# Stationary-weight products that keep to one kind of step for 32 steps instead of 16

## The chip, the cores and the metric

The kernel runs on one core of a Trainium2 chip. The metric is the device time of one execution in microseconds (us); lower is better. A core has five engines that work from queues of their own: PE (the tensor engine, with its weight loads shown apart as PEld), DVE (VectorE), ACT (ScalarE), POOL (GpSimd) and SP, which here only issues DMAs. An engine takes its instructions in the order in which the program put them, and waits on semaphores where it needs another's result.

## The reference

One encoder layer over 256 tokens of width 2048, in float32. Cut to what matters here:

```python
h = rms_norm(x, attn_norm)
qa, ka, va, qb, kb, vb, ga, gb = split(h @ w_in)
ya = windowed_gqa(qa, ka, va, ...)
yb = dilated_attention(qb, kb, vb, ...)
merged = sigmoid(ga) * (ya @ w_branch_a) + sigmoid(gb) * (yb @ w_branch_b)
x = x + merged @ w_out
hf = rms_norm(x, ffn_norm)
g = dwconv_centred(hf @ w_ffn_gate, conv_w, conv_b)
x = x + (gelu(g) * (hf @ w_ffn_up)) @ w_ffn_down
x = x + sigmoid(rms_norm(x, ple_norm) @ w_ple_gate) * (p @ w_ple_proj)
return rms_norm(x, final_norm)
```

The weights are the bulk of the input: all of them are read from memory once, and each is used for 256 tokens.

## The kernel before

**Numbers in two halves.** Products are made in a rounded float32 (fp32r). To keep the precision, each operand is split in two: a high half, the rounded value, and a low half, what the rounding lost. A product is high x high + high x low + low x high.

**Where the halves come from.** The weights are stored as one long stream of blocks of 128 x 128, in the order of use. SP's queue loads them (L265) into six raw buffers; a buffer holds a piece of eight blocks. `split_to(i)` (L276) makes the halves of the pieces up to number i: ACT copies the raw piece, rounding it, into `whi` (L288), and DVE subtracts that from the raw one into `wlo` (L289). `whi` and `wlo` have four buffers each, so the halves of piece s + 4 go where those of piece s were. `load_all` keeps the loads five to six pieces ahead of the split.

**The products with stationary weights.** `product` (L379) makes 128 columns of the q, k, gate (g) or up (u) projections: 16 blocks, two pieces. The weight block is loaded into PE and the activations stream past it. A **high step** (L396) takes a block of `whi` against both halves of the activations, 512 columns; a **low step** (L399) takes a block of `wlo` against their high half, 256 columns, and adds to the second half of the same accumulator. For each piece `eight` (L385) runs eight high and eight low steps: the first piece of a product high ones first, the second low ones first. So the order of kinds in a product is 8 high, 16 low, 8 high, and with the next product behind it, the high ones join to 16. At the start of each piece `split_to(s + 3)` asks for the halves of two pieces ahead. There are 115 such products among the 1840 steps of each kind: q and k ahead of and among the attention, three gate products, and the gate and up products in turn, in two halves of the MLP with the down projection between them.

**The gate products by halves.** The first three gate products (`products_by_halves`, L403) run side by side: the first piece of all three, then the second piece of all three, because the last features are finished only then. The first pieces are all high-first, the second ones low-first.

**What else stands in the order.** `run_due(i, k)` runs what was left for job i at count k: in a product, k goes from 0 to 15, one count for two steps. The scores of an attention head (`scores`, L696) stand at count 9 of the job after its last projection, the transposes of its normalized scores (`turn`, L739) at count 11 or 12 one job later. In the MLP, DVE and ACT work off each finished product: `gather` (L517, L513) adds the accumulator's halves; for a gate product the convolution follows (L846, L849), for every second up product the product with the gate and the sums for the down projection (L860, L863, L873 to L879). DVE also adds up quarters of later weights (`sums_of_quarters`, L322) that POOL's queue loads for it two jobs ahead. A scheduler places the instructions of each engine by its own estimates, so the order on DVE is not quite that of the code.

All other products (the value projections, the branch, output, down and embedding gates) have moving weights (L424 to L426, L475 to L477) and are not touched.

Of the kernel before, what the change touches and what calls it, by code (L numbers as in the profile page):

```python
# [17 lines left out]
T = 256  # L18
# [19 lines left out]
SUB = 8  # L38
# [102 lines left out]
def _pairs(kind, c):  # L141

    if kind == "pgs":
        return [0, 1, 4, 5, 2, 6, 7, 3], range(4, 8)
    if kind == "v8":
        return [0, 1, 2, 4, 3, 5, 6, 7], FARS
    if kind == "gab":
        return [0, 4, 1, 2, 6, 3, 5, 7], GATED
    if kind == "o":
        return ([2, 4, 5, 6, 7, 0, 1, 3] if c else [0, 1, 2, 4, 5, 6, 7, 3]), range(LATER, LATER + 4)  # L150
    if kind == "d1" and c == 1:
        return [5, 0, 1, 6, 2, 3, 7, 4, 8, 9, 10], range(5)
    return [8, 0, 1, 2, 3, 9, 4, 5, 6, 7, 10], range(SAVED)
# [38 lines left out]
def _whole(a):  # L192

    if _BLOCKS[a][0] == "w_in":
        return a == _SEVEN[3]
    pair, first = _BLOCKS[a + SUB][1] % FHALF // 2, not _BLOCKS[a + SUB][2]
    return _BLOCKS[a][0] in ("w_out", "w_ple_gate") or pair in WHOLE or (first and pair == 1)
# [15 lines left out]
_SUB_OF = {a + o: (i, o) for i, (a, n, part) in enumerate(_SUBS) if not part for o in range(n)}  # L213
# [3 lines left out]
def _encoder(ctx: ExitStack, tc, xt, pt, cols, table, onehot, mask, ident_in, last_gain, wts, xrows, out):  # L217
    nc = tc.nc
# [33 lines left out]

    raws, subs = {}, {}
    pairs_of, kept = {}, {}
    state = {"raw": 0, "sub": 0, "at": 0, "back": 0}
    held = {}

    def load(r, a=0, b=PIECE):
# [9 lines left out]
    def load_all(i):  # L268
        while state["raw"] < min(i, 2 * _NPIECES):
            r, h = divmod(state["raw"], 2)  # L270
            seven = h and r * PIECE in _SEVEN
            load(r, h * SUB, h * SUB + (4 if seven else SUB))
            if seven and _whole(r * PIECE):
                nc.sync.dma_start(raws[2 * r + h][:, 4:, :], kept[_SEVEN.index(r * PIECE)][1])

    def split_to(i):  # L276
        while state["sub"] < min(i, len(_SUBS)):
            s = state["sub"]
            a, n, part = _SUBS[s]
            h, o = divmod(a, SUB)  # L280
            load_all(h + 6 + (part == 3))
            if part is None:
                src = raws[h][:, o:min(o + n, SUB), :]
            else:
                src = (raws[h + 1][:, :4, :], pairs_of.get(a), raws[h], raws[h + 1])[part]
            hi = wpool.tile(list(src.shape), FR, name="whi", bufs=4)
            lo = wpool.tile(list(src.shape), FR, name="wlo", bufs=4)
            nc.scalar.activation(hi, src, AF.Copy)  # L288
            ins = nc.vector.tensor_tensor(lo, src, hi.bitcast(F32), op=ALU.subtract)  # L289
            if a // PIECE * PIECE in _EIGHT:  # L290
                keep(ins)
            subs[s] = (hi, lo)
            state["sub"] = s + 1
            if part is not None:
                t2, t4 = raws[h + 1][:, 4:, :], raws[h + 1][:, :4, :]
            if part == 0 and not _whole(a):
                keep(nc.vector.tensor_tensor(t2, raws[h][:, :4, :], pairs_of[a][:, :4, :], op=ALU.add))
            if part == 1:
                keep(nc.vector.tensor_tensor(t4, raws[h][:, 4:, :], t2, op=ALU.add))
                j = _SEVEN.index(a)  # L300
                if all(not j <= e < j + (3 if j > _ENDS["gab"] else 2) for e in _LAST):
                    back()
# [49 lines left out]
    def back():  # L352

        j = state["back"]
        t = two_sums() if "ff" in held else ap_.tile([P, SUB, P], F32, name="sums", tag="near", bufs=2)
        pairs_of[_SEVEN[j]] = t
        nc.sync.dma_start(t, kept[j][0])
        state["back"] = j + 1
# [19 lines left out]

    def product(i, moving, n):  # L379
        acc = ps.tile([P, 2 * T], F32, name="acc", bufs=3)  # L380
        for g in range(n // SUB):
            eight(acc, lambda k: run_due(i, SUB * g + k), lambda k: moving(SUB * g + k), g == 0, g == n // SUB - 1)
        return acc

    def eight(acc, due_at, moving, first, last):  # L385

        s, _ = _SUB_OF[state["at"]]
        for p in range(2 * SUB):
            if p % 2 == 0:
                due_at(p // 2)  # L390
                split_to(s + 3)
            hi, lo = subs[s]
            k = p % SUB
            m = moving(k)
            if (p < SUB) == first:
                nc.tensor.matmul(acc, hi[:, k, :], m, start=(first and k == 0), stop=(last and k == SUB - 1),  # L396
                                 skip_group_check=True)
            else:
                nc.tensor.matmul(acc[:, T:], lo[:, k, :], m[:, :T], start=False, stop=False, skip_group_check=True)  # L399
        state["at"] += SUB  # L400
        del subs[s]

    def products_by_halves(i, moving):  # L403

        accs = []
        for g in range(2 * TOGETHER):
            h, e = divmod(g, TOGETHER)
            if h == 0:
                tag = "sp" if e < 2 else "acc"
                accs.append(ps.tile([P, 2 * T], F32, name="acc", tag=tag, bufs=2 if e < 2 else 3))  # L410
            eight(accs[e], lambda k: run_due(i, SUB * g + k), lambda k: moving(SUB * h + k), h == 0, h == 1)
        return accs

    def wide_product(i, still, n, w, tag, places=HALVES, late=0):

        accs = [ps.tile([P, W4], F32, name="acc", tag=tag, bufs=3 if tag == "acc" else 2) for _ in places]

        def step(k, t, hi, lo):
            xh, xl = (still(k)[:, c:c + T][:, places[t]] for c in (0, T))
            acc = accs[t][:, :w * P]
            nc.tensor.matmul(acc, xh, hi, start=(k == 0), stop=False)  # L424
            nc.tensor.matmul(acc, xh, lo, start=False, stop=False)  # L425
            nc.tensor.matmul(acc, xl, hi, start=False, stop=(k == n - 1 - t * late))  # L426

        later = []
        for k in range(n):
            run_due(i, k)  # L430
            b = state["at"]
            s, o = _SUB_OF[b]
            split_to(s + 3)
            hi, lo = (m[:, o:o + w, :] for m in subs[s])
            step(k, 0, hi, lo)
            if k < n - late:
                step(k, 1, hi, lo)
            else:
                later.append((k, 1, hi, lo))
            state["at"] = b + w  # L440
            if o == _SUBS[s][1] - w:
                del subs[s]
        def rest(side=None):
            acc, c = (accs[1][:, :T], 0) if side is None else (side, T // P)
            for e, (k, t, hi, lo) in enumerate(later):
                xh, xl = (still(k)[:, c:c + T][:, places[t]] for c in (0, T))
                for i, (xs, ws) in enumerate(((xh, hi), (xh, lo), (xl, hi))):
                    nc.tensor.matmul(acc, xs, ws[:, c:c + T // P, :], start=(side is not None and e + i == 0),  # L448
                                     stop=(e + i == len(later) + 1), skip_group_check=True)
        return accs, rest  # L450
# [133 lines left out]
    def run_due(*i):  # L584
        for f, a in due.pop(i, []):
            f(*a)
# [554 lines left out]
    for i, job in enumerate(_JOBS):  # L1141
        kind, n, _, _, _, blocks = job
# [99 lines left out]
        last = i == len(_JOBS) - 1  # L1242
        rest = None
        if kind == "v":
            acc, _ = wide_product(i, stills["v"], blocks, len(n), "acc")
        elif kind in ("o", "d0", "d1", "gab", "pgs", "v8"):
# [21 lines left out]
            def first_gate(bank, k):  # L1268
# [4 lines left out]
            acc = seven_product(i, *_pairs(kind, n), still, lambda m, e: [a[:, e, :] for a in sums_at(m)], tags,  # L1273
                                first_gate if (kind, n) == ("gab", 0) else
                                (lambda bank, k: combined(bank, th)) if kind in ("gab", "pgs", "v8") else
                                (lambda bank, k: spread_sums(kind, n, bank, end, [(i, k), (i, k), (i, k + 1), (i, k + 1)] if end else
                                                             [(i, k), (i, k + 1), (i + 1, 0), (i + 1, 1)])))
        elif kind in stills:
            tag = {"pg": ("acc", "pt"), "pp": ("sp", "acc"), "ba": ("acc", "sp" if n == 1 else "acc"), "bb": ("pt" if n == 0 else "sp", "pt" if n == 1 else "acc")}[kind][n % 2]
            acc, rest = wide_product(i, stills[kind], blocks, 4, tag, late=8 if last else 0)  # L1280
        elif kind == "gg":
            acc = products_by_halves(i, movers["g"])
        else:
            acc = product(i, movers[kind], blocks)
# [13 lines left out]
        elif kind in ("gab", "pgs", "v8"):  # L1298
            th = held["th", "pp" if kind == "pgs" else n]
            for name, a, t in (("p2", "ga", 0), ("p3", "gb", 0), ("p4", "ga", 1), ("c22", "gb", 1)):  # L1300
# [9 lines left out]
                if n == 0 and a == "ga":  # L1310
                    m = held["m"][:, t, :]
# [3 lines left out]
        elif kind in ("o", "d0", "d1"):  # L1315
            parts = held["ss1" if kind == "o" else "ss2"]
# [79 lines left out]
```

## Time and profile before

| | |
|---|---|
| median of 3 runs | 1439.68 us (1439.2 to 1440.29) |
| profiled execution | 1439.28 us, its span 1437.5 us |
| PE busy | 1427.6 us, 99% of the span |
| DVE, ACT, POOL busy | 1181.6 (82%), 876.0 (61%), 182.8 us (13%) |
| high steps, low steps | 1840 of each, 441.1 and 242.1 us |
| DMA | 398.62 MB, mean 277 GB/s |

The span runs from the first to the last instruction of the profiled execution. A row of the page's costliest groups has: line, engine, operation, tile written <- tiles read, shapes, count, then busy time and mean duration, then the idle time of the engine just ahead of these instructions and who ended it. A row of the timeline has: start, duration, engine, line, operation, and how many equal instructions were merged. The durations of matmuls overlap (a row's us reaches past the start of the next), so PE's pace is read from start to start. In rows of waits stand the total, the number of waits and the longest one.

### The profile page before, as it was taken

To read this page: it belongs to the slowest core of one execution; us is meant where nothing else is said; L and a number is where in the kernel's file an instruction comes from. 1 tells how busy PE (TensorE), PEld (TensorE's weight loads), DVE (VectorE), ACT (ScalarE), POOL (GpSimd) and SP (SyncE) were. 2 spreads that over 40 slices of the span, in tenths; PEclk is the share of its full clock that TensorE was granted. 3 is DMA by queue.
4 is the path that set the end of the run, shared out by engine and by line. 5 is a ranking of instruction groups with operands and counts; after the bars stand their busy time and mean duration, and the time that the engine had idled before them with its cause. 6 is when DMAs were issued, how large, how long until landed. Compare 5 with 4: busy or idle time off the path is not lost.

```text
span 1437.5 us, 21024 instructions
## 1 busy us (share of the span) xinstructions
PE 1427.6 (99%) x7452; PEld 1227.9 (85%) x7452; DVE 1181.6 (82%) x1630; ACT 876.0 (61%) x1256; POOL 182.8 (13%) x293
## 2 busy tenths in 40 slices
PE   9999999999999999999999999999999999999997
PEld 8998888888888888888888888888888888888886
DVE  7798966669879978978888878997888887998886
ACT  7576654456656656765555556776555555677864
POOL 0012211220211110101111100102111110010000
PEclk9999999999999999999999999999999999999999
DMA  9798999989989898969888887989898989799672
GB/s 330 250 263 243 310 284 265 255 245 309 277 268 313 256 290 300 287 229 308 298 284 301 288 302 250 284 276 309 292 318 293 316 293 330 250 293 289 212 240 93
DMA packets 128821, 398.62 MB, mean 277 GB/s; under 512 B 14724, under 2 KB 20228, under 8 KB 128588
## 3 DMA queue, kind: packets, MB, share of 16 engines
q1 hardware_dynamic: 93948, 301.64, 60.6%
q0 software_dynamic: 32752, 91.77, 24.6%
q10 hardware_dynamic: 2016, 3.88, 0.9%
q8 instruction: 58, 0.95, 0.3%
q14 instruction: 47, 0.39, 0.1%
HBM read 364.42 MB, written 59.81 MB: 295 GB/s over the span
## 4 chain that ended last, share of the span: by engine, by line
PE 99%; ACT 0%; DMA 0%; DVE 0%; issue 0%; ACTq 0%; DVEq 0%
PE acc L396 29%; PE acc L399 15%; PE acc L475 13%; PE acc L476 13%; PE acc L477 13%; PE acc L424 3%; PE acc L426 3%; PE acc L425 3%; PE first L373 3%; PE pt L748 0%; PE pt L981 0%; PE acc L448 0%; PE sp L705 0%; PE misc L763 0%; PE pt L1020 0%; DMA x<-in_xt 0%
## 5 line engine op out<-in xcount | busy, mean ns | idle before, releaser
L289 DVE TENSOR_TENSOR wlo<-raw,whi 128x1024 fp32r<-128x1024 f32 (+2 forms) x581 | 661.0, 1159 | 99.1 <-ACT whi L288 91.3
L288 ACT ACTIVATE whi<-raw 128x1024 fp32r<-128x1024 f32 (+2 forms) x581 | 572.5, 1005 | 231.6 <-PE acc L477 108.8
L396 PE MATMUL acc<-mov,whi 128*128 128x512 f32 x1840 | 441.1, 391 | 0.0
L396 PEld LDWEIGHTS acc<-mov,whi 128*128 128x128 f32 x1840 | 337.7, 188 | 65.3
L399 PEld LDWEIGHTS acc<-mov,wlo 128*128 128x128 f32 x1840 | 237.1, 191 | 8.8
L399 PE MATMUL acc<-mov,wlo 128*128 128x256 f32 x1840 | 242.1, 283 | 0.0
L513 ACT ACTIVATE t<-acc 128x256 f32<-128x256 f32 x115 | 43.5, 378 | 127.8 <-PE acc L396 127.8
L477 PE MATMUL acc<-whi,mov 128*128 128x512 f32 x259 | 100.8, 389 | 0.0
L476 PE MATMUL acc<-wlo,mov 128*128 128x512 f32 x259 | 100.8, 389 | 0.0
L475 PE MATMUL acc<-whi,mov 128*128 128x512 f32 x259 | 100.6, 390 | 0.0
L289 DVE TENSOR_TENSOR wlo<-sums,whi 128x1024 fp32r<-128x1024 f32 x62 | 75.7, 1220 | 6.6 <-ACT whi L288 6.6
L475 PE MATMUL acc<-whi,act 128*128 128x512 f32 x207 | 80.8, 390 | 0.0
L476 PE MATMUL acc<-wlo,act 128*128 128x512 f32 x207 | 80.6, 390 | 0.0
L477 PE MATMUL acc<-whi,act 128*128 128x512 f32 x207 | 80.6, 389 | 0.0
L288 ACT ACTIVATE whi<-sums 128x1024 fp32r<-128x1024 f32 x62 | 65.5, 1057 | 23.3 <-PE acc L477 11.9
L928 POOL DMA_DIRECT2D x<-row x31 | 26.8, 918 | 301.1 <-PE acc L477 105.6
L475 PE MATMUL acc<-whi,merged 128*128 128x512 f32 x164 | 64.1, 391 | 0.0
L477 PE MATMUL acc<-whi,merged 128*128 128x512 f32 x164 | 63.9, 389 | 0.0
L476 PE MATMUL acc<-wlo,merged 128*128 128x512 f32 x164 | 63.8, 389 | 0.0
L326 POOL DMA_DIRECT2D kept<-sums x33 | 17.8, 538 | 357.7 <-DVE sums L322 212.6
L851 ACT ACTIVATE c<-c 128x256 f32<-128x256 f32 x44 | 18.3, 417 | 68.9 <-DVE c L849 68.9
L477 PEld LDWEIGHTS acc<-whi,mov 128*128 128x128 f32 x259 | 48.6, 188 | 10.2
(274 smaller groups left out, 2144.2 us busy)
## 6 DMA issues: line engine op xcount, KB each, us to landing
raw<-in_wts SPq DMA_DIRECT2D x452, 512.0 KB, 6.2
sums<-kept SPq DMA_DIRECT2D x62, 512.0 KB, 5.8
kept<-in_wts POOLq DMA_DIRECT2D x67, 256.0 KB, 8.1
sums<-in_wts POOLq DMA_DIRECT2D x33, 512.0 KB, 7.6
kept<-sums POOLq DMA_DIRECT2D x33, 512.0 KB, 4.4
raw<-in_wts SPq DMA_DIRECT2D x64, 256.0 KB, 5.2
kept<-in_wts POOLq DMA_DIRECT2D x29, 512.0 KB, 7.7
row<-in_wts POOLq DMA_DIRECT2D x33, 256.0 KB, 8.4
```

What stands on the lines that cost most here:

```text
L288: nc.scalar.activation(hi, src, AF.Copy)
L289: ins = nc.vector.tensor_tensor(lo, src, hi.bitcast(F32), op=ALU.subtract)
L373: nc.tensor.matmul(firsts[e][:, T * low:], w, m[:, :2 * T - T * low], start=(k == 0 and not low), stop=(k == KC - 1 and low != turned), sk ...
L396: nc.tensor.matmul(acc, hi[:, k, :], m, start=(first and k == 0), stop=(last and k == SUB - 1), skip_group_check=True)
L399: nc.tensor.matmul(acc[:, T:], lo[:, k, :], m[:, :T], start=False, stop=False, skip_group_check=True)
L424: nc.tensor.matmul(acc, xh, hi, start=(k == 0), stop=False)
L425: nc.tensor.matmul(acc, xh, lo, start=False, stop=False)
L426: nc.tensor.matmul(acc, xl, hi, start=False, stop=(k == n - 1 - t * late))
L475: nc.tensor.matmul(acc, xh, hi, start=(e == 1), stop=False)
L476: nc.tensor.matmul(acc, xh, lo, start=False, stop=False)
L477: nc.tensor.matmul(acc, xl, hi, start=False, stop=(e == uses[name]))
L513: keep(nc.scalar.activation(t, acc[:, T:], AF.Copy, scale=scale))
```

## The change

`product` no longer works piece by piece. It takes all 16 steps of one kind over both pieces, then all 16 of the other. A variable `low` says which comes first, and turns over from product to product as long as products follow one another directly; behind any other job it starts with high ones. The halves are asked for by a small table `made`, by step number, instead of at the start of each piece. In the gate products by halves, every second piece begins with its low steps.

```diff
     def product(i, moving, n):
         acc = ps.tile([P, 2 * T], F32, name="acc", bufs=3)
-        for g in range(n // SUB):
-            eight(acc, lambda k: run_due(i, SUB * g + k), lambda k: moving(SUB * g + k), g == 0, g == n // SUB - 1)
+        s, _ = _SUB_OF[state["at"]]
+        low = state["low"] if state["job"] == i - 1 else 0
+        made = {0: s + 2, 16: s + 4, 28: s + 5} if low else {0: s + 3, 8: s + 4, 24: s + 5}
+        for p in range(2 * n):
+            if p % 2 == 0:
+                run_due(i, p // 2)
+            split_to(made.get(p, 0))
+            one_step(acc, subs[s + p % n // SUB], p % SUB, moving(p % n), (p < n) == low, p == 0, p == 2 * n - 1)
+        state.update(job=i, low=1 - low, at=state["at"] + n)
+        del subs[s], subs[s + 1]
         return acc
 
-    def eight(acc, due_at, moving, first, last):
+    def one_step(acc, parts, k, m, low, start, stop):
+
+        c = T * low
+        nc.tensor.matmul(acc[:, c:], parts[low][:, k, :], m[:, :2 * T - c], start=start, stop=stop, skip_group_check=True)
+
+    def eight(acc, due_at, moving, first, last, turned):
...
-            if (p < SUB) == first:
-                nc.tensor.matmul(acc, hi[:, k, :], m, start=(first and k == 0), stop=(last and k == SUB - 1),
-                                 skip_group_check=True)
-            else:
-                nc.tensor.matmul(acc[:, T:], lo[:, k, :], m[:, :T], start=False, stop=False, skip_group_check=True)
+            one_step(acc, subs[s], k, moving(k), (p < SUB) == turned, first and p == 0, last and p == 2 * SUB - 1)
...
-            eight(accs[e], lambda k: run_due(i, SUB * g + k), lambda k: moving(SUB * h + k), h == 0, h == 1)
+            eight(accs[e], lambda k: run_due(i, SUB * g + k), lambda k: moving(SUB * h + k), h == 0, h == 1, g % 2)
```

The rest of the diff is the two new entries `job` and `low` of `state`. Below the change all line numbers grow by 7: L322 stays, L517 becomes L524, L860 becomes L867, L879 becomes L886. High and low steps are both on L396 after it.

**First place: PE, an up and a gate product in the second half of the MLP.** The tiles `whi` and `wlo` carry buffer numbers, one pair of neighbouring numbers a piece. Before:

```order
L396 MATMUL acc_10973<-mov_6005,whi_10918 128x512 x8
L399 MATMUL acc_10973<-mov_6005,wlo_10919 128x256 x8
L399 MATMUL acc_10973<-mov_6005,wlo_10945 128x256 x8
L396 MATMUL acc_10973<-mov_6005,whi_10944 128x512 x8
L396 MATMUL acc_11022<-mov_6005,whi_10976 128x512 x8
L399 MATMUL acc_11022<-mov_6005,wlo_10977 128x256 x8
L399 MATMUL acc_11022<-mov_6005,wlo_10999 128x256 x8
L396 MATMUL acc_11022<-mov_6005,whi_10998 128x512 x8
```

The same two products after:

```order
L396 MATMUL acc_10979<-mov_6005,whi_10897 128x512 x8
L396 MATMUL acc_10979<-mov_6005,whi_10944 128x512 x8
L396 MATMUL acc_10979<-mov_6005,wlo_10898 128x256 x8
L396 MATMUL acc_10979<-mov_6005,wlo_10945 128x256 x8
L396 MATMUL acc_11028<-mov_6005,wlo_10963 128x256 x8
L396 MATMUL acc_11028<-mov_6005,wlo_10991 128x256 x8
L396 MATMUL acc_11028<-mov_6005,whi_10962 128x512 x8
L396 MATMUL acc_11028<-mov_6005,whi_10990 128x512 x8
```

The low steps of the two products stand together, 32 in a row; the gate product (the second) begins with low steps, on both of its pieces.

**Second place: DVE, ahead of that pair.** The L322 rows are one group of added-up quarters, `sums` and `row` its tiles; L517 and L846 (L524 and L853 after) are the gather of a product and the first row of the convolution. Before:

```order
L289 TENSOR_TENSOR wlo_10855<-raw_10705,whi_10854 128x1024
L322 TENSOR_TENSOR sums_10758<-sums_10758 128x512
L322 TENSOR_TENSOR sums_10758<-row_10759,sums_10758 128x512
L322 TENSOR_TENSOR row_10759<-row_10759,sums_10758 128x512
L517 TENSOR_TENSOR u_10843<-acc_10796,t_10841 128x256
L846 TENSOR_TENSOR edges_98<-u_10843,rms_9790 128x2x128
L289 TENSOR_TENSOR wlo_10884<-raw_10737,whi_10883 128x1024
```

And after:

```order
L289 TENSOR_TENSOR wlo_10876<-raw_10723,whi_10875 128x1024
L856 SCALAR_TENSOR_TENSOR c_10851<-edges_98,cl_70,c_10851 128x256 x2
L322 TENSOR_TENSOR sums_10758<-sums_10758 128x512
L322 TENSOR_TENSOR sums_10758<-row_10759,sums_10758 128x512
L289 TENSOR_TENSOR wlo_10898<-raw_10762,whi_10897 128x1024
L322 TENSOR_TENSOR row_10759<-row_10759,sums_10758 128x512
L524 TENSOR_TENSOR row_10798<-acc_10857,t_10909 128x256
```

The same group of quarters now stands behind the convolution and behind one more low half (wlo_10876, the piece of wlo_10884 before), and directly ahead of the first low half of the pair above, wlo_10898, and around it.

**Third place: DVE, within that pair.** L860 to L879 (L867 to L886 after) are the work on a pair of up products. Before, from the low half of the up product's second piece to that of the gate product's:

```order
L289 TENSOR_TENSOR wlo_10945<-raw_10797,whi_10944 128x1024
L863 TENSOR_TENSOR act_9702<-row_10792,act_9702 128x2x256
L873 TENSOR_TENSOR row_10909<-row_10792 128x2x128
L289 TENSOR_TENSOR wlo_10977<-raw_10819,whi_10976 128x1024
L875 SCALAR_TENSOR_TENSOR row_10909<-row_10909,row_10792 128x128
L876 TENSOR_TENSOR row_10909<-row_10792,row_10909 128x128
L879 TENSOR_TENSOR shl_6140<-row_10909,shl_6140 128x4x128
L517 TENSOR_TENSOR u_10966<-acc_10915,t_10964 128x256
L846 TENSOR_TENSOR edges_98<-u_10966,rms_9790 128x2x128
L289 TENSOR_TENSOR wlo_10999<-raw_10852,whi_10998 128x1024
```

And after:

```order
L289 TENSOR_TENSOR wlo_10945<-raw_10784,whi_10944 128x1024
L867 TENSOR_TENSOR row_10798<-row_10798,c_10617 128x512
L880 TENSOR_TENSOR row_10915<-row_10798 128x2x128
L882 SCALAR_TENSOR_TENSOR row_10915<-row_10915,row_10798 128x128
L870 TENSOR_TENSOR act_9702<-row_10798,act_9702 128x2x256
L883 TENSOR_TENSOR row_10915<-row_10798,row_10915 128x128
L289 TENSOR_TENSOR wlo_10963<-raw_10819,whi_10962 128x1024
L886 TENSOR_TENSOR shl_6140<-row_10915,shl_6140 128x4x128
L524 TENSOR_TENSOR u_10972<-acc_10921,t_10970 128x256
L289 TENSOR_TENSOR wlo_10991<-raw_10837,whi_10990 128x1024
```

Nearly the same rows stand between the two low halves as before; the first row of the convolution went behind the second one, and the whole product with the gate is now between the first two.

More of the change, by code (lines that the diff above doesn't have):

```diff
@@ L254, in _encoder @@
     pairs_of, kept = {}, {}
-    state = {"raw": 0, "sub": 0, "at": 0, "back": 0}
+    state = {"raw": 0, "sub": 0, "at": 0, "back": 0, "job": 0, "low": 0}
     held = {}
@@ L391, in eight @@
                 split_to(s + 3)
-            hi, lo = subs[s]
             k = p % SUB
-            m = moving(k)
-            if (p < SUB) == first:
-                nc.tensor.matmul(acc, hi[:, k, :], m, start=(first and k == 0), stop=(last and k == SUB - 1),
-                                 skip_group_check=True)
-            else:
-                nc.tensor.matmul(acc[:, T:], lo[:, k, :], m[:, :T], start=False, stop=False, skip_group_check=True)
+            one_step(acc, subs[s], k, moving(k), (p < SUB) == turned, first and p == 0, last and p == 2 * SUB - 1)
         state["at"] += SUB
```

## The prediction, written before the changed kernel ran

> **What bounds the kernel now.** I read the page first (busy times, chain, costliest groups), then the view of waits, then the windows by stage, and last the timeline of single stretches.
>
> ```profile
> span 1437.5 us, 21024 instructions
> ...
> PE 1427.6 (99%) x7452; PEld 1227.9 (85%) x7452; DVE 1181.6 (82%) x1630; ACT 876.0 (61%) x1256; POOL 182.8 (13%) x293
> ...
> PE 99%; ACT 0%; DMA 0%; DVE 0%; issue 0%; ACTq 0%; DVEq 0%
> ...
> L289 DVE TENSOR_TENSOR wlo<-raw,whi 128x1024 fp32r<-128x1024 f32 (+2 forms) x581 | 661.0, 1159 | 99.1 <-ACT whi L288 91.3
> ...
> L396 PE MATMUL acc<-mov,whi 128*128 128x512 f32 x1840 | 441.1, 391 | 0.0
> ...
> L399 PE MATMUL acc<-mov,wlo 128*128 128x256 f32 x1840 | 242.1, 283 | 0.0
> ```
>
> The tensor engine is busy in 99% of the span and is 99% of the chain that ended last. The steps that the change moves are the 1840 high ones (L396) and the 1840 low ones (L399), 683 us together. No time stands ahead of either (the 0.0 at the end of the rows). So nothing is to be won from waits. A gain can only come from the spacing of the steps themselves; a loss comes as soon as a low half (wlo, made by DVE at L289, 1.16 us each) is not there when a step wants it. The windows say how full DVE is in the two halves of the gated MLP, where most of these products run:
>
> ```profile
> core 0: us, PE busy (x) PEld busy (x) DVE busy (x) ACT busy (x) POOL busy (x), PEclk, DMA share, GB/s
> 615.00:870.00 255.00, 255.00 (x1463) 225.02 (x1462) 207.04 (x313) 144.32 (x216) 30.48 (x56) 1.00 0.82 281
> 955.00:1218.00 263.00, 263.00 (x1491) 231.47 (x1490) 218.01 (x316) 149.43 (x216) 39.59 (x69) 1.00 0.90 303
> ```
>
> The clock is 1.00 and PE has no idle time in either. DVE works 207 of 255 us in the first half, 218 of 263 in the second (83%).
>
> **What a change of kind costs.** The timeline of PE gives the start of each run of equal steps. The first four rows are from the gate products by halves (runs of 8), the other four from the second half of the MLP (runs of 16, since the last 8 of a product and the first 8 of the next are of one kind):
>
> ```profile
> 629.25 2.00 PE L396 MATMUL acc<-mov,whi 128*128 128x512 f32 x8
> 631.09 1.11 PE L399 MATMUL acc<-mov,wlo 128*128 128x256 f32 x8
> 632.04 2.00 PE L396 MATMUL acc<-mov,whi 128*128 128x512 f32 x8
> 633.88 1.12 PE L399 MATMUL acc<-mov,wlo 128*128 128x256 f32 x8
> ```
>
> ```profile
> 1100.39 3.82 PE L396 MATMUL acc<-mov,whi 128*128 128x512 f32 x16
> 1104.04 2.08 PE L399 MATMUL acc<-mov,wlo 128*128 128x256 f32 x16
> 1105.95 3.82 PE L396 MATMUL acc<-mov,whi 128*128 128x512 f32 x16
> 1109.61 2.08 PE L399 MATMUL acc<-mov,wlo 128*128 128x256 f32 x16
> ```
>
> From start to start, 8 high steps take 1.84 us and 16 take 3.655 (mean of 3.65 and 3.66). The 8 more cost 1.815, so 0.227 each, and a run of high steps costs 1.84 - 8 x 0.227 = 0.025 us once at its beginning. For low steps 8 take 0.95 and 16 take 1.91: 0.119 each, and nothing (0 to -0.01 us) for a run. One pair of runs less is therefore worth 0.015 to 0.025 us. In the built programs I count 117 changes from low to high before and 60 after; 57 x 0.015 to 0.025 is **0.9 to 1.4 us saved**. Against it, the attention's small matmuls, which stand at fixed counts inside a product, now return to a high step 19 times instead of 8. Each such return begins a run: 11 x 0.025 = 0.3 us. I take 0.9 us net. The kernel cannot get more from this source: all 117 changes together cost under 3 us.
>
> At a length of 32 steps I have no row. By the Trainium skill (TensorE: Matmul & The Clock Gate, "Back-to-back issue gap") the spacing of a stream of small matmuls is set by the weight load and the matmul together, so a long run of short steps could fall to the pace of the weight load, which a short run hides behind the 512-wide steps before it. Here the low steps keep 0.119 us in runs of 8 and of 16 alike, so this trace does not bear it out; were it so, runs of 32 would lose what the first step of a run gains, at most the 0.01 us above.
>
> **When the halves are wanted.** Take a pair of products, the first high-first, the second low-first, two pieces of eight blocks in each. Before, the low halves were wanted at 1.82, 2.77 (first product), 7.39 and 8.34 us (second; 5.57 a product, from 16 x 0.227 + 16 x 0.119 + 0.025). After, they are wanted at 3.63, 4.59, 5.54 and 6.50: the first two 1.8 us later, **the last two 1.84 us earlier**, all four in a row 0.955 us apart (8 x 0.119). DVE needs 1.16 us for one, and its other rows stand between them: at the third place of the order shown ahead, two rows stand between the third and the fourth half, of the kinds L879 and L517 (L886 and L524 in the numbers after). What such rows take:
>
> ```profile
> 1036.31 0.69 DVE L879 TENSOR_TENSOR shl<-row,shl 128x512 fp32r<-128x512 f32 x1
> 1036.91 0.48 DVE L849 SCALAR_TENSOR_TENSOR c<-edges,cl,c 128x256 f32<-128x256 f32 x1
> ...
> 1040.17 0.42 DVE L517 TENSOR_TENSOR row<-acc,t 128x256 f32<-128x256 f32 x1
> ```
>
> 0.69 and 0.42 us; and a row starts some 0.08 us before the one ahead of it ends (1036.91 against 1037.00).
>
> What margin is there? In the second half of the MLP the low-first products are the gate products. These rows pair, for the six of them with least margin, the DVE row that makes the second piece's low half with the PE run in which it is first used (at the ninth of 16 steps, start + 0.955):
>
> ```profile
> 1035.18 1.22 DVE L289 TENSOR_TENSOR wlo<-raw,whi 128x1024 fp32r<-128x1024 f32 x1
> 1037.24 2.08 PE L399 MATMUL acc<-mov,wlo 128*128 128x256 f32 x16
> ...
> 1089.98 1.22 DVE L289 TENSOR_TENSOR wlo<-raw,whi 128x1024 fp32r<-128x1024 f32 x1
> 1092.91 2.08 PE L399 MATMUL acc<-mov,wlo 128*128 128x256 f32 x16
> ...
> 1146.61 1.22 DVE L289 TENSOR_TENSOR wlo<-raw,whi 128x1024 fp32r<-128x1024 f32 x1
> 1148.58 2.08 PE L399 MATMUL acc<-mov,wlo 128*128 128x256 f32 x16
> ...
> 1168.30 1.22 DVE L289 TENSOR_TENSOR wlo<-raw,whi 128x1024 fp32r<-128x1024 f32 x1
> 1170.84 2.08 PE L399 MATMUL acc<-mov,wlo 128*128 128x256 f32 x16
> ...
> 1180.56 1.22 DVE L289 TENSOR_TENSOR wlo<-raw,whi 128x1024 fp32r<-128x1024 f32 x1
> 1181.98 2.08 PE L399 MATMUL acc<-mov,wlo 128*128 128x256 f32 x16
> ...
> 1191.43 1.22 DVE L289 TENSOR_TENSOR wlo<-raw,whi 128x1024 fp32r<-128x1024 f32 x1
> 1193.11 2.08 PE L399 MATMUL acc<-mov,wlo 128*128 128x256 f32 x16
> ```
>
> Ends against needs: 1036.40 and 1038.20, so 1.79 us; then 2.67, 1.71, 2.28, 1.16 and 1.42. A weight load stands about one step ahead of its matmul (0.12, an estimate from the spacing). If DVE finishes these halves when it did before, PE waits where the margin is under 1.84 + 0.12 = 1.96: 0.17 + 0.25 + 0.80 + 0.54 = **1.8 us, the lower end**. The upper end: the fourth half comes 1.22 + 0.69 + 0.42, less the overlap of 0.08 at three seams, so 2.1 us behind the third, and PE wants it 0.955 behind. With the third just in time the fourth is 1.14 late. Adding 1.14 to the threshold (3.10) gives 1.31 + 0.43 + 1.39 + 0.82 + 1.94 + 1.68 = **7.6 us**. I take one DVE row of 0.69, the nearest size of what the order shifts by; threshold 2.65: 0.86 + 0 + 0.94 + 0.37 + 1.49 + 1.23 = **4.9 us**.
>
> The first half has more air. Its tightest place is this:
>
> ```profile
> 645.62 2.35 DVE L289 TENSOR_TENSOR wlo<-raw,whi 128x1024 fp32r<-128x1024 f32 x2
> 649.86 2.08 PE L399 MATMUL acc<-mov,wlo 128*128 128x256 f32 x16
> ```
>
> The first of the two is done by 646.84 and wanted at 650.82: 3.98 us, so I put nothing there.
>
> The high halves are safer: of a pair, one is wanted 1.9 us earlier, but it is made first, and the table `made` has three pieces under way at a product's end where there were two. The weight loads on SP's queue follow the splits one for one and keep their spacing of about 2.7 us (8 steps of each kind), so I cost the DMA at nothing; its cover is the six raw buffers.
>
> **The attention.** Here the wait of PE for the normalized scores is already bare:
>
> ```profile
> 73.50 0.28 PE L692 MATMUL sp<-kf,qf 128*128 128x256 f32 x1
> ...
> 80.94 0.61 DVE L736 TENSOR_SCALAR s<-s,rd 128x256 f32<-128x256 f32 x2
> 81.44 0.72 PE L748 MATMUL pt<-ident,s 128*128 128x128 f32 x4
> ```
>
> For the second head DVE ends at 81.55, when the transposes have begun at 81.44 and wait for their second half. Score to transpose is 7.94 us here. Counting the same steps in the order after gives 7.3, and for the other heads 6.8 to 10. So this head can cost between 0 (DVE also gets there sooner) and 0.6 us; I take 0.3.
>
> **Sum.** The profiled execution took 1439.28 us (span 1437.5 and 1.8 around it), 0.4 under the median of the three runs. 1439.28 - 0.9 + 4.9 + 0.3 = 1443.6; with the 0.4, **1444.0 us**, 0.3% slower.
>
> **Rivals.** *No stall* (the other side: not slower). Splits stand up to three pieces ahead of PE instead of two; if that lets DVE make the gate products' halves 0.7 to 1 us sooner than before, the lower end of 1.8 us melts too, and what is left is the saving: 1439.68 - 0.9 = 1438.8. It decides at a margin of 1.96 us; for it speaks that before, with two pieces ahead, no margin fell under 1.1 us, against it that DVE's other work is not less.
>
> *DVE waits for memory at the wrong moment.* The views of waits have
>
> ```profile
> DVE wlo L289 <- ACT whi L288: 98.0, 125, 2.5
> ...
> DVE sums L322 <- DMA sums<-in_wts: 10.0, 8, 3.2
> DVE sums L322 <- DMA row<-in_wts: 9.6, 10, 2.0
> ```
>
> DVE takes its rows in order, and at L322 it stood 18 times for a weight load, 19.6 us in all, up to 3.2 at once. In the order after, one of these groups now stands right ahead of and between the four low halves (second place shown). If half of that time, 9.8 us, lands ahead of them and half again is covered by margin, 4.9 us come on top: 1444.0 + 5 = 1449.
>
> *The runs cost more than their starts show*, so that halving them brings over 2.9 us: 57 changes would have to cost 0.05 us each, twice the row. 1436.5 at best.
>
> That the change does not do what it says is ruled out by the order: 60 changes, runs of 32.
>
> **Chances.** Forecast (1440 to 1447) 0.45, no stall 0.32, memory waits 0.20, gain 0.03. A measurement of this kernel can tell about 0.2%, 2.9 us, from no change. Slower by more (over 1442.6): the upper three quarters of the forecast and all of the memory case, 0.55; within: 0.42; faster: 0.03. The range runs from just under the case without a stall, 1438.4, to just over the memory case, 1450.
>
> **What would show it.** In the profile after: low rows in runs of 32 and high ones of 32 with 0.227 and 0.119 a step (right for the saving); PE idle ahead of low steps at the first or ninth step of gate products after 1030 us, released by DVE wlo (right for the forecast), each 0.2 to 1.5 us; none before 870 us. DVE rows L322 waiting longer than 19.6 us would bring the dearer rival; PE without any wait for wlo, and a time under 1439.7, would prove the forecast wrong, and so would waits for high halves or for raw loads.

## The result and the profile after

The changed kernel takes 1461.44 us (median of five runs, 1459.99 to 1463.88), the kernel before 1439.6 (1439.07 to 1440.29). The ratio is 1.0152, with a 95% interval of 1.014 to 1.0163. It is 21.8 us slower; I had said 4.3, and the time lies far outside the range. These lines of the page of the changed kernel stand against those shown of before (line numbers are 7 higher behind the changed functions; both kinds of step are L396 now):

```profile
span 1458.2 us, 21046 instructions
...
PE 1434.4 (98%) x7452; PEld 1231.6 (84%) x7452; DVE 1179.2 (81%) x1630; ACT 881.4 (60%) x1256; POOL 185.7 (13%) x293
...
PE 82%; DMA 7%; DVE 7%; issue 2%; ACT 1%; POOL 0%; SPq 0%; DVEq 0%; ACTq 0%; POOLq 0%
...
L396 PE MATMUL acc<-mov,whi 128*128 128x512 f32 x1840 | 432.8, 390 | 0.0
...
L396 PE MATMUL acc<-mov,wlo 128*128 128x256 f32 x1840 | 240.7, 287 | 13.3 <-DVE wlo L289 13.0
...
L322 DVE TENSOR_TENSOR sums<-sums 128x512 f32<-128x512 f32 x33 | 22.7, 687 | 46.5 <-DMA sums<-in_wts 46.5
```

No engine has more instructions than before, and DVE is busy for 1179.2 us against 1181.6; PE is busy for 6.8 us longer, a part of it at the half clock shown below. What else is new stands at the ends of the rows. PE waits 13 us for low halves (0.0 before), and DVE waits 46.5 us at the first of the three sums of a group of quarters. High halves are never waited for. The chain of waits now runs off PE for 18% of the span, 14% of it through DVE and DMA. That is not 18% lost: in experiment 5 below the chain is off PE for 8% of the span, and the time is that of the kernel before. The view of waits gives the same in pairs (engine and row that waits, what it waits for: us in all, how often, the longest):

```profile
POOL kept L326 <- DVE sums L322: 271.6, 24, 15.4
...
DVE sums L322 <- DMA sums<-in_wts: 46.5, 12, 6.5
...
PE acc L396 <- DVE wlo L289: 13.0, 12, 3.3
...
DVE sums L322 <- DMA row<-in_wts: 9.0, 12, 1.7
```

DVE's waits for quarters are 46.5 + 9.0 = 55.5 us, where the kernel before has 19.6. The worst place shows how that reaches PE. The timeline of DVE, start and length of each row, with the wait ahead of it in brackets:

```profile
1041.26 0.68 DVE L322 TENSOR_TENSOR sums<-sums 128x512 f32<-128x512 f32 x1
...
1043.13 0.68 DVE L322 TENSOR_TENSOR row<-row,sums 128x512 f32<-128x512 f32 x1
...
1047.93 0.42 DVE L524 TENSOR_TENSOR row<-acc,t 128x256 f32<-128x256 f32 x1
1054.80 0.69 DVE L322 TENSOR_TENSOR sums<-sums 128x512 f32<-128x512 f32 x1 [6.46 <-DMA sums<-in_wts]
1056.07 0.69 DVE L322 TENSOR_TENSOR sums<-row,sums 128x512 f32<-128x512 f32 x1 [0.58 <-DMA row<-in_wts]
1056.80 0.69 DVE L322 TENSOR_TENSOR row<-row,sums 128x512 f32<-128x512 f32 x1
1057.41 1.22 DVE L289 TENSOR_TENSOR wlo<-raw,whi 128x1024 fp32r<-128x1024 f32 x1
```

One group of sums runs from 1041.26 to 1043.81; the next is reached at 1048.35 (1047.93 + 0.42) and stands there for 6.46 us, because its quarters have not landed. The low half at 1057.41 is behind it in DVE's order. Why the quarters are late is on POOL's timeline, where L326 writes the sums of a group back and L309 and L310 load the next one's quarters:

```profile
1043.28 0.54 POOL L326 DMA_DIRECT2D kept<-sums  x1 [10.75 <-DVE edges L853]
1044.22 0.55 POOL L326 DMA_DIRECT2D kept<-row  x1 [0.40 <-DVE row L322]
1044.79 0.53 POOL L309 DMA_DIRECT2D sums<-in_wts  x1
1045.42 0.55 POOL L310 DMA_DIRECT2D row<-in_wts  x1
```

POOL had been idle for 10.75 us. The load stands behind the writes, and these stand behind DVE's sums. It is issued at 1044.79, and the sums that need it start at 1054.80, 10.0 us later. This is a loop: load, sums, writes, next load. Ten us of load, 2.5 of sums and about 1 to the next load make 13.5 at this place, while a group is due every 2.25 products in this half of the MLP and every 2.5 in the first: by 5.57 us a product 12.5 and 13.9 us, in steps of 2 or 3 products. This load is longer than most. The last table of the page gives medians of 8.2 and 9.2 us from issue to landing for the two transfers of a group (7.6 and 8.4 before), and by the starts of the rows and the landings the whole loop, from a group's first sum until the next group could start, takes 9.2 to 15.3 us here, median 12.2 (before 9.8 to 14.4, median 11.4). By these medians the loop has a slack of 0.3 to 1.7 us at even distances (1.1 to 2.5 before) and none at short ones: when DVE reaches a group early, it stands. PE at the same place:

```profile
1053.34 2.07 PE L396 MATMUL acc<-mov,wlo 128*128 128x256 f32 x16
1058.68 3.86 PE L396 MATMUL acc<-mov,wlo 128*128 128x256 f32 x16 [3.26 <-DVE wlo L289]
```

After a wait of 3.26 us the 16 low steps take 3.86 us, not 2.07: the granted clock is at half there. Such stretches, each 3.41 us long, stand at 836.96, 1058.83 and 1120.27 in the changed kernel, at the ends of its three longest waits, and nowhere in the kernel before from 5.6 us on to its last matmul.

So the sum of the loss is this. From the starts of the steps, PE's 13 waits in the MLP and behind it, counted over a step's own spacing, come to 15.5 us. Three stretches at half clock cost 3 x 3.41 / 2 = 5.1. The saving, measured below, is 0.6. 15.5 + 5.1 - 0.6 = 20.0 of the 20.7 us between the two spans; 0.7 is not assigned. Four of the waits (0.98, 1.14, 2.72 and 0.42 us) and one slow stretch, 7.0 us together, lie in the first half of the MLP.

### The profile page after: what moved, and what is told of

Same layout as the page of the kernel before. It is cut to its first block, busy times and chain, and to the rows that moved or that the text cites. A ratio compares the mean times of both kernels' runs of the same rounds, so it can differ in the third digit from the quotient of the medians.

```text
span 1458.2 us, 21046 instructions
## 1 busy us (share of the span) xinstructions
PE 1434.4 (98%) x7452; PEld 1231.6 (84%) x7452; DVE 1179.2 (81%) x1630; ACT 881.4 (60%) x1256; POOL 185.7 (13%) x293
## 4 chain that ended last, share of the span: by engine, by line
PE 82%; DMA 7%; DVE 7%; issue 2%; ACT 1%; POOL 0%; SPq 0%; DVEq 0%; ACTq 0%; POOLq 0%
PE acc L396 29%; PE acc L482 12%; PE acc L483 12%; PE acc L484 12%; DMA row<-in_wts 6%; PE acc L431 3%; PE acc L433 3%; PE acc L432 3%; DVE wlo L289 3%; PE first L373 2%; DVE sums L322 1%; ACT whi L288 1%; DMA raw<-in_wts 1%; PE pt L755 1%; PE pt L988 0%
## 5 line engine op out<-in xcount | busy, mean ns | idle before, releaser
L396 PE MATMUL acc<-mov,whi 128*128 128x512 f32 x1840 | 432.8, 390 | 0.0
L396 PEld LDWEIGHTS acc<-mov,whi 128*128 128x128 f32 x1840 | 340.5, 188 | 67.4
L396 PE MATMUL acc<-mov,wlo 128*128 128x256 f32 x1840 | 240.7, 287 | 13.3 <-DVE wlo L289 13.0
L396 PEld LDWEIGHTS acc<-mov,wlo 128*128 128x128 f32 x1840 | 234.2, 194 | 21.4 <-DVE wlo L289 16.5
L288 ACT ACTIVATE whi<-sums 128x1024 fp32r<-128x1024 f32 x62 | 65.6, 1058 | 26.7 <-PE acc L484 14.4
L854 ACT ACTIVATE c<-edges,cl 128x256 f32<-128x256 f32 x44 | 26.4, 602 | 87.3 <-DVE edges L853 86.9
L326 POOL DMA_DIRECT2D kept<-sums x33 | 17.8, 538 | 388.3 <-DVE sums L322 271.6
L322 DVE TENSOR_TENSOR sums<-sums 128x512 f32<-128x512 f32 x33 | 22.7, 687 | 46.5 <-DMA sums<-in_wts 46.5
```

The costliest lines, as they stand in the source:

```text
L322: keep(nc.vector.tensor_tensor(dst, p, q, op=ALU.add))
L396: nc.tensor.matmul(acc[:, c:], parts[low][:, k, :], m[:, :2 * T - c], start=start, stop=stop, skip_group_check=True)
```

## The experiments

Two theories stood against each other. In the **bunch theory** the four low halves wanted in a row are too much for DVE, as the forecast had it. In the **memory theory** the sums came to stand elsewhere among DVE's rows, the loop above turned that into waits, and the low halves are late only because DVE stands in front of them.

**1. The loads out of the loop.** Each load of quarters but the first of each series is put one product earlier. Where two groups stand two products apart, the load so goes ahead of the writes of the group before on POOL; where they stand three apart, it follows them within the same product:

```diff
-                sums_ahead((j, 4), (j + 2, 4))
+                sums_ahead((j - (e > 0), 4), (j + 2, 4))
```

> The changed kernel, with the loads of the quarters (the two transfers that the sums of L322 wait for) put one job earlier, 5.57 us; the sums themselves stay where they are. Bunch theory (the low halves are wanted in a row, and DVE's work is too much for that, whatever memory does): PE's waits for wlo stay near 13 us, at least 5 us, and the time stays over 1450 us. Memory theory (the sums, placed later, send the next loads off later, and DVE then stands for them ahead of low halves): DVE's waits at L322, 55.5 us in the changed kernel, fall under 25 us, PE's waits for wlo under 2 us, no stretch of the clock at 0.5 is left after 600 us, and the time is 1438 to 1441 us.

Measured: 1439.01 us against 1439.45, ratio 0.9997 (0.9988 to 1.0005). The page's chain and the row of the low steps, and the POOL timeline at the place shown above:

```profile
PE 99%; DMA 0%; ACT 0%; DVE 0%; SPq 0%; issue 0%; DVEq 0%; ACTq 0%
...
L396 PE MATMUL acc<-mov,wlo 128*128 128x256 f32 x1840 | 232.6, 283 | 0.0
```

```profile
1039.95 0.53 POOL L326 DMA_DIRECT2D kept<-sums  x1 [5.18 <-DVE sums L322]
1040.67 0.54 POOL L326 DMA_DIRECT2D kept<-row  x1 [0.19 <-issue]
1041.24 0.54 POOL L309 DMA_DIRECT2D sums<-in_wts  x1
1041.81 0.55 POOL L310 DMA_DIRECT2D row<-in_wts  x1
1042.37 0.53 POOL L309 DMA_DIRECT2D sums<-in_wts  x1
```

Two loads now follow on one pair of writes; the second of them no longer stands behind the writes of the group before its own. From the issue of a load to DVE's arrival at its sums there are at least 9.9 us, against 3.3 in the changed kernel. DVE never waits at L322, PE never for wlo, and the clock stays up. The whole loss is gone while the four low halves are wanted just as close together. The bunch theory falls here. Slower transfers are not the cause either: the medians from issue to landing are 9.0 and 9.8 us here, longer than in the changed kernel, and nothing is lost.

**2. The bunch taken away.** Every whole product high-first, so that no product begins with low steps; the table of pieces made ahead stays:

```diff
-        low = state["low"] if state["job"] == i - 1 else 0
+        low = 0
```

> The changed kernel with every whole product high-first: runs of 16, no low-first products; the bunch of four low halves is gone, the rest (pieces made ahead by the new table, gate products by halves in turn) stays. Bunch theory: PE does not wait for wlo (under 1 us), 1439 to 1441 us. Memory theory: DVE's waits at L322 depend on where the sums come to stand; if they stay over 40 us while PE waits for wlo under 2 us, memory alone does not do it and the bunch is needed too; 1439 to 1444 us.

Measured: 1450.85 us, ratio 1.008 (1.0066 to 1.0093), more than either theory had said. The view of waits:

```profile
DVE sums L322 <- DMA sums<-in_wts: 51.5, 16, 4.9
...
DVE sums L322 <- DMA row<-in_wts: 4.3, 6, 1.3
...
PE acc L396 <- DVE wlo L289: 3.6, 4, 2.1
```

Without any low-first product DVE stands for 51.5 + 4.3 = 55.8 us and 11 us are lost. From the first high step to the last matmul the trace has 1381.60 us against 1371.23 before; 5.3 of these 10.4 us are PE's waits, counted from the starts of the steps, and 3.4 a stretch of 6.83 us at half clock. The bunch is not needed for a loss. It makes it larger at most: for nearly the same waits of DVE, PE waits 3.6 us for low halves here and 13.0 in the changed kernel. How much of that difference is the bunch's, no run shows.

**3. Where the loss sits.** The gate and up products by eights as before, the rest changed:

```diff
     def product(i, moving, n):
...
+        if _JOBS[i][0] in ("g", "u"):
+            for g in range(n // SUB):
+                eight(acc, lambda k: run_due(i, SUB * g + k), lambda k: moving(SUB * g + k), g == 0, g == 1, g)
+            return acc
```

> The changed kernel with the gate and up products of the MLP taken by eights as before; changed stay the attention, the gate products by halves and the rest. Both theories: the loss sits in the gate and up products, so 1438.5 to 1441 us; DVE's waits at L322 back near 20 us and PE's waits for wlo under 1 us. If the attention costs what I put on it, 0.3 us, the trace up to the end of the attention is that much later than before.

Measured: 1439.68 us, ratio 1.0002 (0.9993 to 1.0011), DVE's waits at L322 6.0 + 9.7 us, none of PE for wlo. The loss sits in the gate and up products, as both theories said.

**4. The first half alone.** The same edit with another condition, so that only the products up to the middle of the MLP are changed:

```diff
+        if i >= _HALF:
```

> The changed kernel with the products from the second half of the MLP on taken by eights as before, the first half changed. My forecast put the first half at nothing: 1438.5 to 1440 us. The trace of the changed kernel shows three waits of PE for wlo there (1.1, 1.3 and 2.8 us) and one stretch of the clock at 0.5: 1445 to 1449 us.

Measured: five runs from 1443.61 to 1452.59, median 1451.01, ratio 1.0063 (1.0043 to 1.0082). The forecast's "nothing" for the first half is wrong, and the loss by itself is even above the 7 us read from the trace of the changed kernel. Its runs are 9 us apart, where the kernels without a loss keep within 3 us and the others that lose time within 5. That would fit a loop with little slack, where a load that lands 1 us sooner decides whether PE waits; no run shows it.

**5. The same loop, other places.** Loads and sums both at step pair 10 of their product instead of 4. The loads stay behind the writes:

```diff
-                sums_ahead((j, 4), (j + 2, 4))
+                sums_ahead((j, 10), (j + 2, 10))
```

> The changed kernel with the loads of the quarters and the sums both put at step pair 10 of their product instead of 4. The loads still stand behind the writes of the group before on POOL's queue; what changes is the place of the sums among the low halves on DVE. In the changed kernel DVE comes to the groups of sums 6.5 to 24 us apart, in the kernel before 9.4 to 17 us, and every interval under 10 us ends in a wait. Interval theory (the chain load, sums, write, next load has no slack, so uneven places become waits): with even places the waits at L322 fall under 30 us, PE does not wait for wlo, 1438 to 1441 us. If it is the bunch, or loads that stand behind writes whatever the places, the time stays over 1450 us.

Measured: 1439.36 us against 1439.6, ratio 0.9997 (0.9988 to 1.0006). The view of waits:

```profile
DVE sums L322 <- DMA sums<-in_wts: 10.5, 9, 2.7
...
DVE sums L322 <- DMA row<-in_wts: 6.7, 11, 1.8
```

and the chain on the page:

```profile
PE 92%; DMA 4%; DVE 2%; issue 1%; ACT 0%; POOL 0%; DVEq 0%; ACTq 0%; POOLq 0%
```

DVE waits 17.2 us at L322. No matmul is shown as waiting for wlo; weight loads (PEld) are, once for 0.3 us in these products and five times, 1.9 us in all, in the down projection. The steps, their runs of 32 and the loop are those of the changed kernel. Only the places of the sums among DVE's rows differ, and with them those of the loads behind their writes.

**6. Uneven places in the kernel before.** The products by eights, as they were, with the sums of every second group late, and the load behind them too:

```diff
-                sums_ahead((j, 4), (j + 2, 4))
+                sums_ahead((j, 14 if e % 2 else 4), (j + 2, 4 if e % 2 else 14))
```

> The kernel before, products by eights, with every second group of quarters put at step pair 14 instead of 4 (its sums and the load after them alike), so that the groups come at uneven distances, about 3.5 us nearer and farther in turn. Interval theory: DVE's waits at L322, 19.6 us in the kernel before, go over 60 us, PE waits for wlo over 8 us, and the time is over 1452 us although no step of the products is changed. If the eights had enough margin and long runs were needed for the loss, the time stays under 1443 us.

Measured: 1472.63 us, ratio 1.0225 (1.0211 to 1.0239). The waits of this kernel (its low steps are L399, as in the kernel before):

```profile
DVE sums L322 <- DMA sums<-in_wts: 60.3, 16, 8.1
...
PE acc L399 <- DVE wlo L289: 20.2, 6, 5.9
...
DVE sums L322 <- DMA row<-in_wts: 6.4, 11, 1.1
```

The kernel before, with no step of a product touched, loses more than the change did. The edit also shortens the way from every second load to its sums, from 32 counts to 22; in this loop, where a load follows on the sums before, that and a short distance between groups are one thing. The table sorts the intervals from DVE's arrival at one group of sums (the start of its first row less the wait) to that at the next; the 33 groups lie in two series, so there are 31 intervals. In each cell: how many intervals, and the us that DVE then stood at the second group's first row.

| kernel | under 10 us | 10 to 14 us | over 14 us | time, us |
|---|---|---|---|---|
| before | 2: 2.7 | 19: 7.2 | 10: 0 | 1439.6 |
| changed | 9: 40.9 | 8: 3.8 | 14: 1.8 | 1461.44 |
| 2, high first | 8: 33.2 | 10: 14.0 | 13: 4.3 | 1450.85 |
| 5, sums at 10 | 2: 1.0 | 19: 9.6 | 10: 0 | 1439.36 |
| 6, before, uneven | 16: 60.3 | 0 | 15: 0 | 1472.63 |
| 1, early loads | 5: 0 | 14: 0 | 12: 0 | 1439.01 |

Experiment 5 has before's spread of intervals and its time; experiment 6 has more short ones than the changed kernel and a larger loss. The last line closes the argument: five short intervals, 5.4 to 5.9 us, without any wait, since there the load does not follow on the sums. (The ranges of intervals in the expectation of experiment 5 were a first reading. By these rows they are 9.2 to 19.5 us before and 6.6 to 23.7 after.)

**7. Early loads in the kernel before**, the edit of experiment 1, as its control.

> The kernel before with the loads of the quarters one job earlier. There PE never waits for wlo, so both theories say no change: 1439.0 to 1440 us, with DVE's waits at L322 near 0 instead of 19.6 us. The distance to the changed kernel with early loads (1439.01) is what the change brings when no wait follows: 0.4 to 0.9 us by my terms.

Measured: 1439.9 us against 1439.6, ratio 1.0002 (0.9993 to 1.001), DVE's waits at L322 down to one of 0.3 us. Before, they cost nothing. Against this control the changed kernel with early loads shows the change's own worth. The times, 0.9 us apart with intervals of over 1 us, cannot settle it, but PE has no waits in either trace. From the first row of the high steps to the last matmul, in the control:

```profile
57.39 2.00 PE L396 MATMUL acc<-mov,whi 128*128 128x512 f32 x8
...
1428.59 0.28 PE L448 MATMUL acc<-whi,mov 128*128 128x256 f32 x1
```

and in experiment 1:

```profile
58.18 1.55 PE L396 MATMUL acc<-mov,whi 128*128 128x512 f32 x6
...
1428.82 0.28 PE L455 MATMUL acc<-whi,mov 128*128 128x256 f32 x1
```

1371.20 against 1370.64 us: the change saves 0.56 us when no wait follows. Each is one execution; the kernel before, whose steps are those of the control, gives 1371.23. A version that beats the kernel before by an amount that can be measured is not among these.

## Why the prediction was wrong

The step that failed is the largest term of the sum, 4.9 us for low halves that are wanted earlier: it cost nothing. In its place stands the loop of loads and sums, which the rival had at 5 us and which cost 20.6 us (15.5 of waits and 5.1 of half clock). That the kernel came out slower, as forecast, is luck: the forecast's reason for it is not the cause.

**The saving was right.** 0.9 from fewer runs less 0.3 for the attention's second head makes 0.6; the traces give 0.56. The attention is there too: to its end (the first matmul that reads its result, counted from the first high step) the control takes 343.51 us and experiment 1 343.84, 0.33 more. Experiment 3, which keeps the change in the attention and not in the MLP, takes 1371.59 us from the first high step to the last matmul, 0.36 more than the kernel before. Runs of 32 have the spacing that the short ones had, here in experiment 1:

```profile
1093.01 7.44 PE L396 MATMUL acc<-mov,whi 128*128 128x512 f32 x32
1100.29 4.00 PE L396 MATMUL acc<-mov,wlo 128*128 128x256 f32 x32
1104.12 7.44 PE L396 MATMUL acc<-mov,whi 128*128 128x512 f32 x32
```

Start to start 7.28 = 32 x 0.227 + 0.025, and 3.83 for 32 low steps, 0.120 each: no fall to a slower pace. The rule weighed there (the Trainium skill, TensorE: Matmul & The Clock Gate, "Back-to-back issue gap") does not bite in this kernel.

**The shift of the low halves was wrong, all 4.9 us of it.** "If DVE finishes these halves when it did before" was the assumption, and it failed: the table `made` puts three pieces ahead of PE, and DVE finishes sooner. In experiment 1, with the same shift, it even stands for PE to free its buffers, as the row below shows; the changed kernel has 14.6 us of such waits, the kernel before and the control none:

```profile
DVE wlo L289 <- PE acc L396: 25.7, 26, 2.0
```

In experiment 1 PE does not wait for low halves at all. That is the rival "no stall", priced at 1438.8; with the loads out of the loop it came out at 1439.01. Its lower end, 1.8 us, should have been weighed with that lead in, not beside it. (The upper end of 7.6 us also left out two places, with margins of 2.72 and 2.99 us under its threshold of 3.10; with them it is 8.1.)

**The memory rival had the mechanism and a wrong size.** Its step was "if half of that time, 9.8 us, lands ahead of them and half again is covered by margin, 4.9 us". It took before's 19.6 us as a fixed store that the change deals out anew. But the waits are made by the places: the groups' distances on DVE went from two under 10 us to nine, and the waits to 55.5. The profile of before held what was needed. Its view of waits shows POOL standing at the writes for these sums:

```profile
POOL kept L326 <- DVE sums L322: 212.6, 19, 15.8
```

The next load stands behind these writes in POOL's order. A group's period of 12.5 or 13.9 us against the loop's median of 11.4 leaves 1.1 to 2.5 us. I read one place of the order, and so saw the group move; I did not read the distances of all 33. Why the scheduler places the groups so unevenly in the changed kernel was not traced. That PE then waits 13 to 15.5 us was not in the sum.

**The first half of the MLP was put at nothing** on the strength of its air, 3.98 us at the tightest place. That air was measured with DVE's waits where they were. DVE's waits there are now up to 5.6 us long, and one of those in front of a low half uses it up. This half lost 7.0 us, and experiment 4 more.

**The clock was not in it.** 5.1 us of the loss is PE running at half speed after its waits. PE never waits that long in the MLP of before, so no row there priced it.

**What would show it** said: PE idle ahead of low steps after 1030 us, each 0.2 to 1.5 us, none before 870. The releaser was right; four waits stand before 870, and three are longer than 2.4 us. "DVE rows L322 waiting longer than 19.6 us would bring the dearer rival" was the sign that came.

The high halves and the weight loads on SP's queue, costed at nothing, did cost nothing (0.0 at the row of the high steps).

## What to carry to other kernels

Where an engine that works in order also waits for a transfer, ask what starts that transfer. If it is the engine's own earlier result, the loop's time against the period at which it is asked for is a bound like any other, and with little slack in it even a harmless move of the work between becomes a wait in front of whatever stands behind. So when a change moves instructions, list the distances between all rows of such a loop before and after, not the order at one place. The simplest cure tried here was to take the next load out from behind the result, one product earlier: it removed the waits in both kernels (experiments 1 and 7), whatever the order.

## What the runs showed of the hardware

In these traces PE's clock falls in steps of a fixed raster. The stretches at half clock ahead of the last matmul last 3.41 or 6.83 us, and their starts within one trace lie whole multiples of 3.413 us apart (in the changed kernel 1058.83 to 1120.27 is 18 of them, 836.96 to 1058.83 is 65). By every such stretch here, what decides is how busy PE was in the cell of the raster (one stretch of 3.413 us) just ended, not how long a wait was. The windows view laid on that raster (PE busy is the second number, the granted clock stands behind POOL), first of the changed kernel:

```profile
core 0: us, PE busy (x) PEld busy (x) DVE busy (x) ACT busy (x) POOL busy (x), PEclk, DMA share, GB/s
720.91:724.32 3.41, 1.86 (x13) 1.66 (x14) 3.34 (x7) 1.58 (x2) 1.40 (x3) 1.00 0.64 185
724.32:727.73 3.41, 3.41 (x19) 2.88 (x19) 3.41 (x6) 0.90 (x2) 0.00 (x0) 1.00 0.99 358
...
1116.86:1120.27 3.41, 1.15 (x10) 0.95 (x9) 3.29 (x7) 3.31 (x5) 0.08 (x1) 1.00 0.82 256
1120.27:1123.68 3.41, 3.08 (x15) 2.78 (x14) 2.70 (x6) 2.52 (x4) 0.00 (x0) 0.50 1.02 346
```

then of experiment 6:

```profile
746.16:749.57 3.41, 0.00 (x0) 0.00 (x0) 3.06 (x7) 0.83 (x3) 0.54 (x1) 1.00 0.09 37
749.57:752.98 3.41, 2.15 (x9) 2.16 (x10) 3.41 (x7) 1.04 (x3) 1.64 (x3) 0.50 0.75 274
752.98:756.40 3.42, 3.42 (x9) 2.65 (x9) 3.38 (x6) 2.15 (x3) 0.00 (x0) 0.50 0.90 285
...
1104.56:1107.98 3.42, 2.24 (x14) 1.84 (x12) 2.35 (x5) 0.00 (x0) 0.54 (x1) 1.00 0.60 238
1107.98:1111.39 3.41, 2.14 (x13) 1.97 (x14) 3.23 (x5) 0.71 (x2) 1.64 (x3) 1.00 0.85 297
```

and of experiment 2:

```profile
1103.91:1107.32 3.41, 1.70 (x11) 1.07 (x9) 3.41 (x6) 0.33 (x1) 1.08 (x2) 1.00 0.37 102
1107.32:1110.73 3.41, 2.58 (x10) 2.48 (x11) 3.41 (x7) 1.52 (x3) 1.09 (x2) 0.50 0.92 328
```

A cell with 1.86 us of PE work keeps the clock, one with 1.70 loses it for the next cell; so do the cells with 1.15 and 0.00, and two with 1.64 in experiment 4. The wait of 2.61 us in experiment 6 (1106.64 to 1109.25) lay across two cells, 2.24 and 2.14 busy, and cost no clock, while one of 2.42 inside a cell of the changed kernel did. To come back takes more: after slow cells with 2.15 and 2.58 us of work, and 2.79 in experiment 4, the next one is slow too, after 3.08 it is fast. The Trainium skill (TensorE: Matmul & The Clock Gate, "What's actually happening") gives a free-running window of 3413 ns, which these starts bear out; its advice to keep idle gaps under about 3.4 us ("HAM oscillation — how this bites in real kernels") is too wide for this kernel, where a gap of 2.42 us was enough. The bounds, about half a cell to fall and 2.79 to 3.08 us to return, are read from these traces and were not tried by themselves.
